# Roots of a norm moved to GpSimd, late additions behind a scaling, and weight splits held back, in a one-core trunk kernel

## The chip, the cores and the metric

The kernel runs on one core of a Trainium2 chip. Times are device microseconds; the metric is the median of several runs. The engines are TensorE (PE in the profile; PEld is its weight load), VectorE (DVE), ScalarE (ACT), GpSimd (POOL) and SyncE (SP), which issues the transfers.

## The reference, cut to what matters

One macaron layer over 1024 rows of 1024 columns, in float32: half a SwiGLU feed-forward, stick-breaking attention, half a SwiGLU feed-forward. Each has a root-mean-square norm in front.

```python
def rms_norm(x, gain):
    y = x * lax.rsqrt(jnp.mean(x * x, axis=-1, keepdims=True) + 1e-6)
    return y * gain

x = x + 0.5 * swiglu(rms_norm(x, l0_ff1_norm), l0_ff1_w_in, l0_ff1_w_out)   # w_in 1024x5632, w_out 2816x1024
x = x + stick_breaking_attention(rms_norm(x, l0_mix_norm), w_qkv, q_gain, k_gain, w_o)   # 16 heads of 64
x = x + 0.5 * swiglu(rms_norm(x, l0_ff2_norm), l0_ff2_w_in, l0_ff2_w_out)
```

The change concerns the second norm, `l0_mix_norm`, between the output product of the first feed-forward and the QKV product.

## The kernel before

Every float32 product is done as three fp32r products (`mm3`, lines 282 to 284): each operand is split into a high part, which ScalarE copies, and a low part, the difference, which VectorE or GpSimd takes (`split`, lines 185 and 186). Rows are handled in eight blocks of 128 ("row 0" to "row 7" below); the order is 4, 5, 6, 7, 0, 1, 2, 3, since the input comes reversed in time.

The output product of a feed-forward (`ffn_out`) is a Strassen-like scheme of seven half-size products, in the order 5, 1, 4, 3, 7, 2, 6 (`SEVEN`). A product has an inner length of 1408, in six chunks (`CHUNKS`): five of two 128-slices, one of one. For each chunk, transfers bring one or two parts of the weight into tiles `raw` and the stored gate product into `rh`; VectorE sums the weight parts where there are two (line 527); the splits write four tiles `rp`. Product 7 accumulates into four PSUM banks ma0 to ma3, product 2 into mb0 to mb3, product 6 again into ma. `result(t)` (line 573) adds a finished bank t, times 0.5 and a sign, into the residual `x_sb`, one addition for each half it goes to. Product 2 goes to two halves, so it has eight additions; they are the late ones: `finish_late` issues them behind a split of product 6's operands, by the table

```python
LATE = ((2, (0, 1)), (4, (2, 3)))
```

banks 0 and 1 behind chunk 2's last split, banks 2 and 3 behind chunk 4's. The last three chunks of product 6 are taken bank by bank (block 0 to block 3).

The hook `at` weaves the norm into these products. A norm of a row takes two squares with a sum on ScalarE (line 221), the sum of both halves `st` (line 230), the root `rsqrt` on VectorE (a scale-and-add, line 195; a first guess by integer arithmetic, line 198; three Newton steps of three instructions, lines 200 to 202), the scaling of the row by root and gain into `xs`, two instructions of 512 columns (line 245), and `turned`: eight transposes on TensorE into two banks (line 257) and the splits into `xh` and `xl`. Rows 4 and 5 are normed after product 7 and turned in product 2; rows 6 and 7 have their root taken in product 2, are scaled behind chunk 4's split of product 6, and are turned in banks mb0 to mb3 after block 0 of product 6. Rows 0 to 3 are normed one by one after blocks 0 to 3; row 0 is turned after block 3, row 1 after the first block of the QKV product, rows 2 and 3 after the fourth.

The QKV product of a head pair accumulates 128 rows by 384 columns in one of two banks `bq`, empties them (`sq`, `qk`, `vst`, lines 774 to 780) and goes on. `weights_of` loads its weights `raw_qkv` in four steps of two slices and splits them into `wqh` (ScalarE, line 742) and `wql` (GpSimd, line 745). The table `behind` names tiles that a step has to wait for: a GpSimd multiply of two columns (line 740) reads such a tile and writes where the split will write. For the first head pair, the first two steps (slices 4 to 7) wait for nothing, the other two for the last `xl` of row 7:

```python
for engine, to, f in behind[n]:
    there = f().to_broadcast([P, 2])
    engine.tensor_tensor((h_, l_)[to][:, ks, 0], there, there, op=ALU.mult)
```

The framework orders the instructions of each engine when the program is built, by the priorities of their place in the text and planned times; `issue_after` adds an edge of order to one engine's queue. At run time each engine goes through its queue in that order.

Of the kernel before, what the change touches and what calls it, by code (L numbers as in the profile page):

```python
# [9 lines left out]
F32 = mybir.dt.float32  # L10
# [3 lines left out]
ALU = mybir.AluOpType  # L14
# [3 lines left out]
P = 128  # L18
T = 1024
D = 1024  # L20
# [7 lines left out]
EPS = 1e-6  # L28
# [56 lines left out]

ON_POOL_H = {2: (1,), 6: (1, 3, 5)}

LATE = ((2, (0, 1)), (4, (2, 3)))

W_OF = {  # L90
    1: ((0, 0), (1, 1), "add"), 2: ((0, 0),), 3: ((0, 1), (1, 1), "subtract"), 4: ((1, 0), (0, 0), "subtract"),
# [17 lines left out]
def macaron_kernel(ctx, tc, x, g1, w1_in, w1_out, gm, w_qkv, gq, gk, w_o, g2, w2_in, w2_out, out):  # L109
    nc = tc.nc  # L110
    act, dve, pool_e, pe, sp = nc.scalar, nc.vector, nc.gpsimd, nc.tensor, nc.sync
# [62 lines left out]
    make_identity(nc, ident)  # L174
    xh = cpool.tile([P, KD, T], F32R, name="xh")
    xl = cpool.tile([P, KD, T], F32R, name="xl")
    above = cpool.tile([P, 104], F32, name="above")
    pool_e.memset(below, 0.0)
    pool_e.memset(above, 0.0)
    x_keep = [dram.tile([T, D], F32, name=f"x_keep{i}") for i in range(2)]  # L180
    o_keep = [dram.tile([NP * P, T], F32, name=f"o_keep{n}") for n in "hl"]

# [6 lines left out]
    def rsqrt(pool, ss, inv_n, y=None):  # L189
# [12 lines left out]
            dve.scalar_tensor_tensor(out=y, in0=u, scalar=1.5, in1=y, op0=ALU.subtract, op1=ALU.mult)  # L202
        return y

    def load_gain(pl, g):

        t = pl["xs"].tile([P, D], F32, name="gain", bufs=1)
        sp.dma_start(t, g.broadcast_to([P, D]))
        return t
# [10 lines left out]
                junk = pl["hs"].tile([P, NHALF], F32, name="hs", bufs=1)  # L220
                act.activation(junk, row(tb, h), AF.Square, accum_out=ss[:, i, h : h + 1])

    def rates(pl, row, tbs, ss=None):

        n = len(tbs)
        if ss is None:
            ss = pl["xs"].tile([P, n, 2], F32, name="ss")
            squares(pl, row, tbs, ss)
        st = pl["xs"].tile([P, n], F32, name="st")
        dve.tensor_tensor(st, ss[:, :, 0], ss[:, :, 1], op=ALU.add)  # L230
        return rsqrt(pl["xs"], st, 1.0 / D)

    def norm(pl, row, tbs, gain, ss=None, r=None, behind=None):

        if r is None:
            r = rates(pl, row, tbs, ss)
        turns = []  # L240
        for i, tb in enumerate(tbs):
            xs = pl["xs"].tile([P, D], F32, name="xs")
            with tc.issue_after(behind) if behind is not None else nullcontext():
                for h in range(2):
                    dve.scalar_tensor_tensor(
                        out=xs[:, HALVES[h]], in0=row(tb, h), scalar=r[:, i : i + 1], in1=gain[:, HALVES[h]],
                        op0=ALU.mult, op1=ALU.mult,
                    )
            turns.append(partial(turned, xs, tb))
        return turns  # L250
# [258 lines left out]
    def ffn_out(pl, w_out, keep, x_from, ahead, at):  # L509

        place["rp"] = 0
        x_sb = [pl[f"x{h}"].tile([P, NT, NHALF], F32, name=f"x{h}", bufs=1) for h in range(2)]

        def room(n):
            i = PLACES[place["rp"] % len(PLACES)]
            place["rp"] += 1  # L520
            return pl[f"rp{i}"].tile([P, 2, NHALF], F32R, name="rp", bufs=1)[:, :n]

        def operands(m, c):
            n = len(CHUNKS[c])
            *w, h = ahead.pop((m, c), None) or operand_raw(pl, w_out, keep, m, c)
            if len(w) == 2:
                dve.tensor_tensor(w[0], w[0], w[1], op=getattr(ALU, W_OF[m][2]))  # L527
            wh, wl, hh, hl = (room(n) for _ in range(4))
            marks = *split(w[0], wh, wl, pool_e), *split(h, hh, hl, pool_e if c in ON_POOL_H.get(m, ()) else dve)
            return (wh, wl), (hh, hl), marks  # L530

        def load(th, h):
            for tb in range(4 * (1 - th), 4 * (1 - th) + 4):
                sp.dma_start(x_sb[h][:, tb, :], x_from[rows(tb), HALVES[h]])

        def finish_late(m, result, ops, part):

            c, ts = LATE[part]
            for t in ts:
                with tc.issue_after(ops[c][2][3]):  # L540
                    result(t)
            with tc.issue_after(ops[-1][2][0]), tc.issue_after(ops[-1][2][2]):
                at(x_sb, m, f"end {part}", ops)

        open_banks = {}
        loaded = set()
        for m, tag, fresh, goes in SEVEN:
            last = m == SEVEN[-1][0]
            late = m == SEVEN[-2][0]
            if fresh:  # L550
                open_banks[tag] = [bank(tag) for _ in range(4)]
            bs = open_banks[tag]
            ops = [operands(m, c) for c in range(len(CHUNKS))]
            for (th, h), _ in goes:
                if (th, h) not in loaded:
                    load(th, h)
                    loaded.add((th, h))

            def add(ts, cs):
                for c in cs:  # L560
                    (wh, wl), (hh, hl), _ = ops[c]
                    for i, q in enumerate(CHUNKS[c]):
                        for t in ts:
                            s = slice(t * P, (t + 1) * P)
                            mm3(
                                bs[t], [((hh[:, i, s], hl[:, i, s]), (wh[:, i], wl[:, i]))],
                                fresh and q == 0, q == NQ - 1, not fresh,
                            )

            def result(t, bs=bs, goes=goes):  # L570
                for (th, h), sign in goes:
                    xc = x_sb[h][:, 4 * (1 - th) + t, :]
                    dve.scalar_tensor_tensor(out=xc, in0=bs[t], scalar=0.5 * sign, in1=xc, op0=ALU.mult, op1=ALU.add)

            if last:
                late_result(ops, 0)
            n = len(CHUNKS) - BY_BLOCK if last else len(CHUNKS)
            for c in range(n):
                add(range(4), [c])
                at(x_sb, m, c, ops)  # L580
                if last and c == 0:
                    late_result(ops, 1)
            for t in range(4):
                add([t], range(n, len(CHUNKS)))
                if not late:
                    result(t)
                if last:
                    at(x_sb, m, f"block {t}", ops)
            if late:
                late_result = partial(finish_late, m, result)  # L590
            else:
                at(x_sb, m, "end", ops)
# [25 lines left out]
    pending = []  # L618
    with pools(*RAWS) as pr:
        ops = {}  # L620
# [37 lines left out]
        late, stores = [], []  # L658
        norms = ExitStack()
        pn = norms.enter_context(pools("xs", "hs", side="right"))  # L660
        with banks("ps2"), pools(*SECOND) as pl:
            lay_banks()
            gain_m = load_gain(pn, gm)
            half = pn["xs"].tile([P, 4, 2], F32, name="half", bufs=1)

            def at(x_sb, m, where, ops):
                def row(tb, h):
                    return x_sb[h][:, tb, :]

                def store(tbs, hs):  # L670
                    for tb in tbs:
                        for h in hs:
                            sp.dma_start(x_keep[0][rows(tb), HALVES[h]], row(tb, h))

                def turn_rows(bk, n):
                    for _ in range(n):
                        pending.pop(0)(bk)

                if (m, where) == (7, "end"):
                    pending.extend(norm(pn, row, (4, 5), gain_m))  # L680
                    store((4, 5, 6, 7), (0, 1))
                elif (m, where) == (2, 2):
                    turn_rows("ma", 2)
                elif (m, where) == (2, 3):
                    late.append(rates(pn, row, (6, 7)))
                elif (m, where) == (6, 0):

                    pending.extend(norm(pn, row, (6, 7), gain_m, r=late.pop(), behind=ops[4][2][3]))
                elif m == 2 and str(where).startswith("end"):
                    ts = slice(*((0, 2), (2, 4))[int(where[-1])])  # L690
                    squares(pn, row, range(4)[ts], half[:, ts], (0,))
                elif m == 6 and str(where).startswith("block"):
                    t = int(where[-1])
                    turn_rows("mb", (2, 0, 0, 1)[t])
                    squares(pn, row, (t,), half[:, t : t + 1], (1,))
                    last_norm = lambda: pending.extend(norm(pn, row, (t,), gain_m, half[:, t : t + 1]))
                    if t < 3:
                        last_norm()
                    else:
                        late.append(last_norm)  # L700
                    stores.append(partial(store, (t,), (0, 1)))

            ffn_out(pl | pr, w1_out, keep, x, ops, at)

# [5 lines left out]
    with ExitStack() as stack:  # L710
# [228 lines left out]
        steps = qkv(0, states[0])  # L939

        last_x = ((pool_e, 0, lambda: xl[:, KD - 1, T - P : T - P + 1].bitcast(F32)),)
        for f in weights_of(0, states[0], ((), last_x)):
            f()
        with tc.issue_after(states[0]["loaded"]):
            for f in stores:
# [212 lines left out]
```

## Time and profile before

| | us |
|---|---|
| median of 3 runs | 1951.02 |
| lowest and highest | 1950.53, 1951.62 |
| profiled execution, its own time | 1951.8 |
| its span (first to last instruction) | 1950.0 |
| busy PE, PEld | 1910.0 (98%), 1639.0 (84%) |
| busy DVE, ACT, POOL | 1267.2 (65%), 986.9 (51%), 1092.4 (56%) |
| mean granted clock of TensorE | 0.999 |

A busy share is a mean over stages of different kinds. What the change touches lies between 603 us, where product 2 begins, and about 700 us, where the attention's scores are near; so the stretch and the single waits in it are to be read, and not the shares. In a timeline a line is one group of like instructions: start, duration of the group, engine, line, operation, tile written and tiles read, shape, count, and in brackets the idle time before it and what ended it.

### The profile page before, as it was taken

What the parts mean: (1) busy time and instruction counts of PE and PEld (TensorE: products, weight loads), DVE (VectorE), ACT (ScalarE), POOL (GpSimd) and SP (SyncE); (2) the same over time, 40 slices, a digit from 0 to 9 for tenths busy, and PEclk for the clock granted to TensorE, in tenths of its full rate; (3) what the DMA queues carried; (4) which work ended last, traced back from release to release, by engine and by line L of the source; (5) the groups of instructions that cost most, each with busy time, mean ns of one, the idle gap of its engine ahead of it and who ended that gap; (6) DMA issues with size and microseconds to landing.
All of it is one profiled execution on the core that took longest, in us unless ns stands there. A gap on an engine that the chain in (4) does not pass through costs nothing.

```text
span 1950.0 us, 27326 instructions
## 1 busy us (share of the span) xinstructions
PE 1910.0 (98%) x9656; PEld 1639.0 (84%) x9656; DVE 1267.2 (65%) x1834; ACT 986.9 (51%) x1802; POOL 1092.4 (56%) x963
## 2 busy tenths in 40 slices
PE   7999999999999999999999999999999999999998
PEld 7978888888888898888989897789888888888887
DVE  7855545635876867878787878475645545548644
ACT  6533443344334457777787877344433343343332
POOL 3667667655545636656655664113666666655554
PEclk9999999999999999999999999999999999999999
DMA  6223223338896411011011134521323232369973
GB/s 211 82 92 125 98 97 104 118 114 277 322 344 229 139 34 43 32 43 49 28 39 45 60 114 167 179 70 43 129 87 121 98 103 88 129 211 339 337 267 134
DMA packets 168505, 260.26 MB, mean 133 GB/s; under 512 B 11568, under 2 KB 81200, under 8 KB 168368
## 3 DMA queue, kind: packets, MB, share of 16 engines
q1 hardware_dynamic: 168368, 258.52, 38.8%
q8 instruction: 75, 1.23, 0.3%
q14 instruction: 62, 0.51, 0.1%
HBM read 198.18 MB, written 60.29 MB: 133 GB/s over the span
## 4 chain that ended last, share of the span: by engine, by line
PE 85%; DVE 8%; ACT 3%; issue 2%; POOL 2%; DMA 1%; DVEq 0%; POOLq 0%; ACTq 0%
PE ka L282 6%; PE ka L284 6%; PE ka L283 6%; PE kc L284 4%; PE kc L282 4%; PE kc L283 4%; PE kb L284 4%; PE kb L282 4%; PE kb L283 4%; PE ma L283 4%; PE ma L284 4%; PE ma L282 4%; PE bq L282 4%; PE bq L283 4%; PE bq L284 4%; PE bo L905 3%
## 5 line engine op out<-in xcount | busy, mean ns | idle before, releaser
L186 POOL TENSOR_TENSOR u<-sf,u 128x512 fp32r<-128x512 f32 x160 | 226.1, 1415 | 150.9 <-ACT u L185 147.0
L186 POOL TENSOR_TENSOR rp<-raw,rp 128x1024 fp32r<-128x1024 f32 x84 | 208.9, 2491 | 179.1 <-ACT rp L185 168.3
L186 POOL TENSOR_TENSOR u<-raw,u 128x512 fp32r<-128x512 f32 x136 | 196.2, 1448 | 164.2 <-ACT u L185 162.9
L185 ACT ACTIVATE u<-sf 128x512 fp32r<-128x512 f32 x160 | 100.7, 630 | 214.8 <-PE kb L283 86.8
L865 POOL TENSOR_TENSOR w<-w,om 128x512 f32<-128x512 f32 (+4 forms) x128 | 141.1, 1106 | 114.6 <-DVE om L858 88.3
L401 DVE TENSOR_TENSOR h<-h 128x512 f32<-128x512 f32 x110 | 135.4, 1234 | 85.9 <-POOL h L505 85.1
L282 PE MATMUL bq<-wqh,xh 128*128 128x384 f32 x512 | 174.8, 341 | 2.1 <-DVE vst L779 2.1
L284 PE MATMUL bq<-wqh,xl 128*128 128x384 f32 x512 | 172.2, 336 | 0.0
L283 PE MATMUL bq<-wql,xh 128*128 128x384 f32 x512 | 172.1, 336 | 0.0
L185 ACT ACTIVATE rp<-rh 128x1024 fp32r<-128x1024 f32 (+1 forms) x78 | 76.4, 984 | 188.0 <-issue 57.5
L282 PE MATMUL ka<-xh,u 128*128 128x512 f32 (+1 forms) x448 | 162.2, 362 | 1.5 <-ACT s L453 1.5
L283 PE MATMUL ka<-xl,u 128*128 128x512 f32 (+1 forms) x448 | 162.1, 362 | 0.0
L284 PE MATMUL ka<-xh,u 128*128 128x512 f32 (+1 forms) x448 | 161.9, 361 | 0.0
L527 DVE TENSOR_TENSOR raw<-raw 128x1024 f32<-128x1024 f32 (+1 forms) x60 | 97.6, 1629 | 99.0 <-DMA raw<-w_out 89.1
L185 ACT ACTIVATE u<-raw 128x512 fp32r<-128x512 f32 x136 | 84.9, 631 | 148.9 <-PE ka L283 101.2
L282 PE MATMUL ma<-rp 128*128 128x512 f32 x352 | 137.5, 390 | 0.0
L283 PE MATMUL ma<-rp 128*128 128x512 f32 x352 | 137.2, 390 | 0.0
L284 PE MATMUL ma<-rp 128*128 128x512 f32 x352 | 137.2, 390 | 0.0
L856 ACT ACTIVATE w<-bz,f 128x512 f32<-128x512 f32 (+2 forms) x192 | 112.5, 586 | 41.5 <-PE bz L852 38.9
L505 POOL TENSOR_TENSOR h<-h,g 128x512 f32<-128x512 f32 x80 | 113.0, 1412 | 35.1 <-DVE h L457 33.3
L430 DVE TENSOR_TENSOR sf<-raw 128x512 f32<-128x512 f32 x80 | 81.2, 1015 | 78.0 <-POOL u L186 77.9
L186 DVE TENSOR_TENSOR rp<-rh,rp 128x1024 fp32r<-128x1024 f32 (+1 forms) x70 | 106.2, 1535 | 22.6 <-ACT rp L185 19.7
(272 smaller groups left out, 5557.8 us busy)
## 6 DMA issues: line engine op xcount, KB each, us to landing
raw<-w_out SPq DMA_DIRECT2D x120, 512.0 KB, 5.4
raw<-w_in SPq DMA_DIRECT2D x88, 512.0 KB, 3.6
k<-h SPq DMA_DIRECT2D x154, 256.0 KB, 2.1
rh<-k SPq DMA_DIRECT2D x64, 512.0 KB, 5.8
raw_qkv<-w_qkv SPq DMA_DIRECT2D x64, 192.0 KB, 2.9
x_keep<-x SPq DMA_DIRECT2D x32, 256.0 KB, 3.7
x<-x_keep SPq DMA_DIRECT2D x32, 256.0 KB, 5.2
raw<-w_out SPq DMA_DIRECT2D x24, 256.0 KB, 4.7
```

What stands on the lines that cost most here:

```text
L185: act.activation(hi, raw, AF.Copy).ins,
L186: (engine or dve).tensor_tensor(lo, raw, hi.bitcast(F32), op=ALU.subtract).ins,
L282: pe.matmul(dst, ah, bh, start=start and i == 0, stop=False, skip_group_check=onto)
L283: pe.matmul(dst, ah, bl, start=False, stop=False, skip_group_check=onto)
L284: pe.matmul(dst, al, bh, start=False, stop=stop and i == n - 1, skip_group_check=onto)
L401: dve.tensor_tensor(src, hb[of[0]], hb[of[1]], op=getattr(ALU, of[2]))
L430: dve.tensor_tensor(f[n], x, y, op=op)
L505: pool_e.tensor_tensor(h, h, gs[k], op=ALU.mult)
L527: dve.tensor_tensor(w[0], w[0], w[1], op=getattr(ALU, W_OF[m][2]))
L856: act.activation(to, z, AF.Sigmoid, scale=state["f", half][:, sign, tb % 4, hd : hd + 1])
L865: pool_e.tensor_tensor(wt[:, c1 : c0 + n], wt[:, c1 : c0 + n], om[:, c1 - 1 : c0 + n - 1], op=ALU.mult)
L905: pe.matmul(ot[:, :n], vv, t[:, c : c + n], start=start, stop=stop)
```

## The change

All six roots of this norm (rows 4 and 5 together, 6 and 7 together, 0, 1, 2 and 3) go to GpSimd: the sum `st`, one scale-and-add, and one `tensor_tensor` with `pow` against a constant tile of -0.5 take the place of the twelve VectorE instructions. The other two norms keep `rsqrt`. The tile `above`, which only fills memory, shrinks by 8 columns as the tile `power` comes in. The late additions of banks 0 and 1 go from behind chunk 2's split to behind chunk 4's, and both parts are issued in the text after the scaling of rows 6 and 7. The first two weight steps of the first head pair get a wait on GpSimd for the first late addition of row 0 (`added`). `store` gets `row` as an argument, so that `added` can reach the tile.

```diff
-LATE = ((2, (0, 1)), (4, (2, 3)))
+LATE = ((4, (0, 1)), (4, (2, 3)))
...
-    above = cpool.tile([P, 104], F32, name="above")
+    above = cpool.tile([P, 96], F32, name="above")
+    power = cpool.tile([P, 1], F32, name="power")
...
+    pool_e.memset(power, -0.5)
...
+    def root(pool, ss, inv_n):
+        n = ss.shape[-1]
+        a, y = (pool.tile([P, n], F32, name=f"rs_{i}", bufs=b) for i, b in (("a", 4), ("y", 2)))
+        pool_e.tensor_scalar(a, ss, inv_n, EPS, op0=ALU.mult, op1=ALU.add)
+        pool_e.tensor_tensor(y, a, power.to_broadcast([P, n]), op=ALU.pow)
+        return y
...
-    def rates(pl, row, tbs, ss=None):
+    def rates(pl, row, tbs, ss=None, pooled=False):
...
-        dve.tensor_tensor(st, ss[:, :, 0], ss[:, :, 1], op=ALU.add)
-        return rsqrt(pl["xs"], st, 1.0 / D)
+        (pool_e if pooled else dve).tensor_tensor(st, ss[:, :, 0], ss[:, :, 1], op=ALU.add)
+        return root(pl["xs"], st, 1.0 / D) if pooled else rsqrt(pl["xs"], st, 1.0 / D)
...
-            if last:
-                late_result(ops, 0)
...
-                if last and c == 0:
-                    late_result(ops, 1)
+                if last and c < 2:
+                    late_result(ops, c)
...
-                    pending.extend(norm(pn, row, (4, 5), gain_m))
+                    pending.extend(norm(pn, row, (4, 5), gain_m, pooled=True))
...
-                    late.append(rates(pn, row, (6, 7)))
+                    late.append(rates(pn, row, (6, 7), pooled=True))
...
-                    last_norm = lambda: pending.extend(norm(pn, row, (t,), gain_m, half[:, t : t + 1]))
+                    last_norm = lambda: pending.extend(norm(pn, row, (t,), gain_m, half[:, t : t + 1], pooled=True))
...
-                    stores.append(partial(store, (t,), (0, 1)))
+                    stores.append(partial(store, row, (t,), (0, 1)))
...
-        for f in weights_of(0, states[0], ((), last_x)):
+        added = ((pool_e, 1, lambda: stores[0].args[0](0, 0)[:, 0:1]),)
+        for f in weights_of(0, states[0], (added, last_x)):
```

More of the change, by code (lines that the diff above doesn't have):

```diff
@@ L229, in rates, with norm @@
         st = pl["xs"].tile([P, n], F32, name="st")
-        dve.tensor_tensor(st, ss[:, :, 0], ss[:, :, 1], op=ALU.add)
-        return rsqrt(pl["xs"], st, 1.0 / D)
-    def norm(pl, row, tbs, gain, ss=None, r=None, behind=None):
+        (pool_e if pooled else dve).tensor_tensor(st, ss[:, :, 0], ss[:, :, 1], op=ALU.add)
+        return root(pl["xs"], st, 1.0 / D) if pooled else rsqrt(pl["xs"], st, 1.0 / D)
+    def norm(pl, row, tbs, gain, ss=None, r=None, behind=None, pooled=False):
         if r is None:
-            r = rates(pl, row, tbs, ss)
+            r = rates(pl, row, tbs, ss, pooled)
         turns = []
@@ L668, in row, with store @@
                     return x_sb[h][:, tb, :]
-                def store(tbs, hs):
+                def store(row, tbs, hs):
                     for tb in tbs:
@@ L679, in at @@
                 if (m, where) == (7, "end"):
-                    pending.extend(norm(pn, row, (4, 5), gain_m))
-                    store((4, 5, 6, 7), (0, 1))
+                    pending.extend(norm(pn, row, (4, 5), gain_m, pooled=True))
+                    store(row, (4, 5, 6, 7), (0, 1))
                 elif (m, where) == (2, 2):
```

## The prediction

> **What bounds the kernel now.** I read busy time by stretches first, to see where TensorE does not work; then its waits there; then the timelines of the four engines around each wait. A line of the first view: stretch, us, busy us and instructions of PE, PEld, DVE, ACT and POOL, granted clock, DMA share, GB/s.
>
> ```profile
> 600.00:640.00 40.00, 40.00 (x184) 33.01 (x184) 31.67 (x45) 22.42 (x36) 24.04 (x10) 1.00 0.66 223
> 640.00:700.00 60.00, 55.69 (x294) 49.56 (x293) 49.92 (x112) 26.02 (x58) 31.28 (x30) 0.97 0.35 110
> ...
> 800.00:900.00 100.00, 96.74 (x580) 88.88 (x579) 80.64 (x155) 77.75 (x168) 59.18 (x88) 1.00 0.13 40
> ```
>
> TensorE is the bound: from 600 to 640 us, where the first moved root lies, it never rests; from 640 to 700, where the other edits lie, it idles 60.00 - 55.69 = 4.3 us. Two waits, both for VectorE, make that up (waited for, total us, times, longest):
>
> ```profile
> PE mb L257 <- DVE x L573: 2.2, 2, 1.9
> PE bq L282 <- DVE vst L779: 2.1, 1, 2.1
> ```
>
> On TensorE's timeline (start, duration):
>
> ```profile
> 655.49 1.03 PE L257 MATMUL mb<-ident,xs 128*128 128x128 f32 x8
> 658.41 0.92 PE L257 MATMUL mb<-ident,xs 128*128 128x128 f32 x4 [1.90 <-DVE x L573]
> 659.61 1.11 PE L257 MATMUL mb<-ident,xs 128*128 128x128 f32 x4 [0.27 <-DVE x L573]
> 660.37 0.78 PE L282 MATMUL ma<-rp 128*128 128x512 f32 x1
> ...
> 662.16 0.40 PE L283 MATMUL ma<-rp 128*128 128x512 f32 x1
> 662.40 0.39 PE L284 MATMUL ma<-rp 128*128 128x512 f32 x1
> ...
> 671.48 1.03 PE L257 MATMUL mb<-ident,xs 128*128 128x128 f32 x8
> ...
> 681.22 0.33 PE L283 MATMUL bq<-wql,xh 128*128 128x384 f32 x1
> 681.39 0.34 PE L284 MATMUL bq<-wqh,xl 128*128 128x384 f32 x1
> 683.84 0.45 PE L282 MATMUL bq<-wqh,xh 128*128 128x384 f32 x1 [2.11 <-DVE vst L779]
> ```
>
> Stall 1: the 16 transposes of rows 6 and 7 take banks mb0 to mb3, four each. Eight go at once; mb2 and mb3 wait for the last late additions of product 2. No product runs from 655.49 to 660.37, 4.9 us. Stall 2: the third QKV block wants the bank of the first, which VectorE (vst) empties late; start to start that is 683.84 - 681.39 less the usual 0.17, 2.3 us.
>
> **Part 1, additions behind the scaling, weights' splits held.** VectorE, then GpSimd:
>
> ```profile
> 645.83 2.47 DVE L573 SCALAR_TENSOR_TENSOR x<-mb,x 128x512 f32<-128x512 f32 x4
> 648.23 0.75 DVE L527 TENSOR_TENSOR raw<-raw 128x512 f32<-128x512 f32 x1
> 648.90 2.31 DVE L186 TENSOR_TENSOR rp<-rh,rp 128x1024 fp32r<-128x1024 f32 x1
> 651.14 6.02 DVE L245 SCALAR_TENSOR_TENSOR xs<-x,rs_y,gain 128x512 f32<-128x512 f32 x4
> 657.08 2.47 DVE L573 SCALAR_TENSOR_TENSOR x<-mb,x 128x512 f32<-128x512 f32 x4
> ...
> 668.19 1.41 DVE L245 SCALAR_TENSOR_TENSOR xs<-x,rs_y,gain 128x512 f32<-128x512 f32 x2
> ```
>
> ```profile
> 646.01 2.43 POOL L186 TENSOR_TENSOR rp<-raw,rp 128x1024 fp32r<-128x1024 f32 x1 [2.31 <-ACT rp L185]
> 648.36 1.77 POOL L186 TENSOR_TENSOR rp<-rh,rp 128x512 fp32r<-128x512 f32 x1
> 650.09 2.28 POOL L186 TENSOR_TENSOR rp<-raw,rp 128x512 fp32r<-128x512 f32 x1
> 652.45 5.57 POOL L745 TENSOR_TENSOR wql<-raw_qkv,wqh 128x384 fp32r<-128x384 f32 x4
> 662.85 0.34 POOL L740 TENSOR_TENSOR wqh<-xl 128x2 fp32r<-128x2 f32 x2 [4.84 <-DVE st L230]
> 664.01 3.94 POOL L745 TENSOR_TENSOR wql<-raw_qkv,wqh 128x384 fp32r<-128x384 f32 x4 [0.81 <-ACT wqh L742]
> 677.46 1.69 POOL L740 TENSOR_TENSOR wqh<-qk 128x2 fp32r<-128x2 f32 x4 [9.51 <-ACT qk L775]
> 679.34 3.91 POOL L745 TENSOR_TENSOR wql<-raw_qkv,wqh 128x384 fp32r<-128x384 f32 x4 [0.19 <-ACT wqh L742]
> ```
>
> A scaling (two SBUF tiles in) costs 6.02 / 4 = 1.5 us while GpSimd splits, and 1.41 / 2 = 0.7 at 668.19 while it rests. An addition (one bank, one SBUF tile) costs 2.47 / 4 = 0.62 with GpSimd busy or not. The change puts the additions, not the scaling, beside the first weights' splits.
>
> New order from 645.8: L527 0.75, chunk 4's split 2.31, to 648.9; scaling; eight additions, 8 x 0.62 = 4.9. With scaling at 4 x 0.7 the additions end at 656.6, with 4 x 1.5 at 659.8, against 659.55 now. GpSimd still has chunk 5's two splits, by its rows to 652.4, and after them only the held weights. I take contention till then: 3.5 / 1.5 = 2.35 pieces, 1.65 more at 0.7, so 653.6, and the additions end at 658.5. Four transposes follow, about 0.5 (half of the eight's 1.03) instead of 0.76: products resume at 659.05, **1.3 us earlier**. Between the ends that is 3.2 us and nothing.
>
> Behind the new wait on GpSimd (two multiplies of two columns, 0.34 / 2 = 0.17 each at 662.85) are the four first splits: released at about 654 and uncontended (3.94 for four), they end at 658, as now, so their second loads come no later. The next four wait for xl of row 7, as now, and come with it.
>
> A second gain is the clock:
>
> ```profile
> 659.00:660.00 1.00, 0.73 (x4) 0.39 (x3) 1.00 (x2) 0.95 (x3) 0.00 (x0) 0.50 0.47 129
> ...
> 681.70:683.90 2.20, 0.09 (x2) 0.06 (x1) 2.17 (x5) 0.83 (x3) 1.54 (x2) 1.00 0.44 122
> ```
>
> The 4.9 us without a product ended at half the granted clock; four products from 660.37 took 1.79 in place of 4 x 0.24, **0.8 lost**. The 2.3 us of stall 2 cost no clock. 659.05 - 655.49 = 3.6 lies between the two; I count half, 0.4 (ends 0 and 0.8). The Trainium skill, "TensorE: Matmul & The Clock Gate", section What's actually happening, has the clock halved after an idle window of about 3.4 us that runs free of the program. By that rule a gap of 4.9 would catch a whole window in 1.5 / 3.4 = 0.44 of executions and one of 3.6 in 0.06, an estimate of 0.38 x 0.8 = 0.3 saved on the median, and the sum would be 0.1 longer. The trace agrees as far as it goes: 0.50 after 4.9 us, 1.00 after 2.3.
>
> **Part 2, six roots to GpSimd.** Each takes twelve small instructions from VectorE and puts three on GpSimd. Around stall 2 and the first root:
>
> ```profile
> 613.36 0.15 DVE L230 TENSOR_TENSOR st<-ss 128x2 f32<-128x2 f32 x1
> ...
> 618.83 2.74 DVE L245 SCALAR_TENSOR_TENSOR xs<-x,rs_y,gain 128x512 f32<-128x512 f32 x4
> ...
> 676.66 0.15 DVE L230 TENSOR_TENSOR st<-half 128x1 f32<-128x1 f32 x1
> ...
> 679.47 0.90 DVE L202 SCALAR_TENSOR_TENSOR rs_y<-rs_u,rs_y 128x1 f32<-128x1 f32 x1
> ...
> 683.51 0.28 DVE L779 TENSOR_TENSOR vst<-bq,vst 128x128 fp32r<-128x128 f32 x1
> ```
>
> ```profile
> 677.26 0.28 ACT L778 ACTIVATE vst<-bq 128x128 fp32r<-128x128 f32 x1
> ```
>
> vst's input is there at 677.5; it starts at 683.51 because row 3's root stands before it, its last steps 0.9 us each beside the splits at 679.34. Without the chain vst can run by 679 with row 2's scaling ahead of it, and TensorE asks at 681.6: **2.3 us saved**. Next late would be the second block's vst, asked for one block (4 us) later.
>
> Price on GpSimd: sum and scale-and-add at 0.17 to 0.2; the power is in no row. I take 0.2, the row of the same shape; the upper end is 2.4, its longest operand split here of 1024 columns. A root is then X = 0.6 to 2.8 us. The first root:
>
> ```profile
> 608.95 3.40 POOL L186 TENSOR_TENSOR rp<-raw,rp 128x1024 fp32r<-128x1024 f32 x1 [3.47 <-ACT rp L185]
> 613.53 2.44 POOL L186 TENSOR_TENSOR rp<-raw,rp 128x1024 fp32r<-128x1024 f32 x1 [1.18 <-ACT rp L185]
> ...
> 624.02 2.40 POOL L186 TENSOR_TENSOR rp<-raw,rp 128x1024 fp32r<-128x1024 f32 x1 [5.83 <-ACT rp L185]
> ```
>
> It runs from 612.35, and the four scalings end at 613 + 2.8 = 616 instead of 621.6. Splits behind it shift by X into the 5.8 us idle before 624.02; so does the second root. At 2.8 both still fit. TensorE turns these rows at 620.0, so nothing is gained there either. For rows 0 to 3, blocks end at 662.4, 665.9 and 669.3 (three in 671.48 - 660.37 - 0.8 = 10.3 us): result 0.7, squares 0.8, root 0.6 and scaling 1.4 need 3.5, and TensorE turns row 0 at 669.3, row 1 a QKV block later. The weights' splits at 664.01 may stand behind two of these roots: they end at 667.95 - 1.3 + 2X, and QKV starts at 670.1, so 2X up to 3.4 is free, and 2.2 would be lost at X = 2.8. The memset of one column at the start (no input) and the shorter pad cost nothing; no DMA is added, and the stores keep their places in SP's queue.
>
> The Trainium skill, "GPSIMD Engine Reference", section Instruction dispatch, speaks against this part: the first call of freshly loaded code waits about 6 us. No run here shows it. By that the first root would end at about 619 and the scaling at 620.4 for row 4, an estimate of 0.7 us of TensorE's time lost; the forecast would be 1947.7.
>
> **Sum.** The profiled execution took 1951.8 (span 1950.0), 0.8 above the median 1951.02, and had the clock loss whole: 1951.8 - 1.3 - 0.8 - 2.3 = 1947.4. On the median: 1951.0 - 1.3 - 0.4 - 2.3 = **1947.0**. Everything later hangs on TensorE and shifts with it.
>
> **Rivals.**
> - One stall stays (0.20). VectorE's order is fixed when the program is built; if row 3's scaling comes ahead of vst and its root sits on GpSimd behind the splits of 679.34 to 683.25, stall 2 stays: 1951.0 - 1.7 = 1949.3. For: vst was put last now too. Against: these splits are traced later than the root. If scaling stays contended throughout, stall 1 stays: 1948.7.
> - Nothing comes out (0.10): the attention gives it back, 1951.0. For: TensorE idles 3.3 of 100 us there (800 to 900), in an order that may be planned anew. Against: those waits follow its own products.
> - Slower (0.12): the power is a long program. Past X = 1.7 each us costs 2 before QKV; at X = 3.7 the gain is gone, at 5.7 the time is 1955. Against: the short GpSimd rows of 0.17.
>
> **How the numbers follow.** The forecast has 0.58, its own range 1944.7 (3.2 + 0.8 + 2.3 saved) to 1948.8. About 0.2%, 3.9 us, is what a measurement can tell, so 1947.1 parts faster from same: some six tenths of the forecast's share, 0.37, is faster; its rest, one stall, and nothing make 0.49 same; the long power and a bad new order 0.14. The range 1944.6 to 1952.0 leaves out little below and the long power above.
>
> **What would show it.** Scaling of rows 6 and 7 at 0.7 to 1.1 us a piece, then eight additions in a row; TensorE's wait before the mb transposes under 1 us each, granted clock 1.00 there; no wait of bq for vst at 680; three GpSimd instructions per root at 0.2 each. Wrong if the power shows above 1.7 us, or bq waits for wql or xl.

## The result, and the profile after

The changed kernel takes 1945.95 us (median of 9 runs, 1945.13 to 1947.17), the kernel before 1951.02 on the same chip (9 runs, 1948.92 to 1953.22): a ratio of 0.9974 with an interval of 0.9964 to 0.9984. It takes 5.1 us less, a quarter of a percent, and the interval leaves out no change; the forecast of 1947.0 is 1.1 us above it. The profiled execution took 1945.95 (span 1944.2), against 1951.8 (span 1950.0).

Line numbers have moved: the split is now L188, the scaling L255, the transposes L267, the products L292 to L294, the additions L583, vst L787, the wait and the split of the weights L748 and L753; a root on GpSimd is L240, L211 and L212 (in the runs with more powers most of these are one further). The stretches that bound the kernel, in the columns of the prediction's first view:

```profile
600.00:640.00 40.00, 40.00 (x186) 33.37 (x185) 25.95 (x21) 22.63 (x36) 28.60 (x16) 1.00 0.68 233
640.00:700.00 60.00, 57.70 (x311) 51.41 (x310) 39.80 (x67) 27.18 (x61) 34.35 (x45) 1.00 0.33 103
```

TensorE idles 2.3 us from 640 to 700 where it idled 4.3, at the full granted clock. Its waits there (waited for, total us, times, longest):

```profile
PE mb L267 <- DVE x L583: 1.8, 4, 0.5
PE bt L267 <- DVE xl L188: 0.5, 1, 0.5
```

The wait of bq for vst is gone, the wait of the mb transposes is 1.8 in four pieces instead of 2.2 in two, and one wait is new: the transposes of row 1 (bt) for the splits of row 0. TensorE's timeline, of after and then, at the same places, of before:

```profile
620.88 0.48 PE L292 MATMUL mb<-rp 128*128 128x512 f32 x1
...
654.08 0.39 PE L294 MATMUL ma<-rp 128*128 128x512 f32 x1
654.65 0.66 PE L267 MATMUL mb<-ident,xs 128*128 128x128 f32 x4 [0.18 <-DVE x L583]
...
658.24 0.66 PE L267 MATMUL mb<-ident,xs 128*128 128x128 f32 x4 [0.54 <-DVE x L583]
658.65 0.47 PE L292 MATMUL ma<-rp 128*128 128x512 f32 x1
...
669.77 0.42 PE L292 MATMUL bq<-wqh,xh 128*128 128x384 f32 x1
...
674.68 1.23 PE L267 MATMUL bt<-ident,xs 128*128 128x128 f32 x8 [0.47 <-DVE xl L188]
675.66 0.42 PE L292 MATMUL bq<-wqh,xh 128*128 128x384 f32 x1
...
679.91 0.33 PE L292 MATMUL bq<-wqh,xh 128*128 128x384 f32 x1
```

```profile
622.03 0.47 PE L282 MATMUL mb<-rp 128*128 128x512 f32 x1
...
672.27 0.42 PE L282 MATMUL bq<-wqh,xh 128*128 128x384 f32 x1
...
677.31 0.42 PE L282 MATMUL bq<-wqh,xh 128*128 128x384 f32 x1
```

Subtracting pair by pair gives where the time came from. The turn of rows 4 and 5 begins 0.79 us earlier than before, a lead from ahead of the first moved root; after it (620.88 against 622.03) the lead is 1.15: 0.36 gained in the turn, where the kernel before has 0.4 us of waiting for the scaling and this one none. The products resume 1.72 earlier (658.65 against 660.37), so the gap around the mb transposes gave 0.54 to 0.57. Some 0.35 of that is the clock too: the last four transposes and the step to the first product took 660.37 - 659.61 = 0.76 at half clock before, and 658.65 - 658.24 = 0.41 now. QKV starts 2.50 earlier (669.77 against 672.27): 0.78, the half clock that did not come behind the gap. The second block starts only 1.65 earlier (675.66 against 677.31): 0.85 given back at the turn of row 1. The third block starts 3.93 earlier (679.91 against 683.84): 2.28, stall 2. By the last product the lead is 4.7, by the end of the span 5.8; the last 1.1 lies behind the last product, among the stores. From the start of the last product to the end it is 5.3 us in both profiles of the kernel before and with order and hold alone, and 4.1 to 4.2 in all ten others, one with its roots on VectorE among them; what sets it stays open.

VectorE and GpSimd of after:

```profile
645.26 3.41 DVE L188 TENSOR_TENSOR rp<-rh,rp 128x1024 fp32r<-128x1024 f32 x1
648.60 4.80 DVE L255 SCALAR_TENSOR_TENSOR xs<-x,rs_y,gain 128x512 f32<-128x512 f32 x4
653.32 4.86 DVE L583 SCALAR_TENSOR_TENSOR x<-mb,x 128x512 f32<-128x512 f32 x8
...
668.48 1.41 DVE L255 SCALAR_TENSOR_TENSOR xs<-x,rs_y,gain 128x512 f32<-128x512 f32 x2 [4.30 <-POOL rs_y L212]
669.82 1.28 DVE L583 SCALAR_TENSOR_TENSOR x<-ma,x 128x512 f32<-128x512 f32 x2
672.52 1.42 DVE L255 SCALAR_TENSOR_TENSOR xs<-x,rs_y,gain 128x512 f32<-128x512 f32 x2 [1.42 <-POOL rs_y L212]
673.85 1.28 DVE L188 TENSOR_TENSOR xl<-mb,xh 128x512 fp32r<-128x512 f32 x2
...
675.38 0.28 DVE L787 TENSOR_TENSOR vst<-bq,vst 128x128 fp32r<-128x128 f32 x1
```

```profile
612.77 0.20 POOL L211 TENSOR_SCALAR rs_a<-st 128x2 f32<-128x2 f32 x1
613.05 0.71 POOL L212 TENSOR_TENSOR rs_y<-rs_a,power 128x2 f32<-128x2 f32 x1
...
661.03 0.19 POOL L240 TENSOR_TENSOR st<-half 128x1 f32<-128x1 f32 x1 [1.51 <-ACT hs L231]
661.31 0.19 POOL L211 TENSOR_SCALAR rs_a<-st 128x1 f32<-128x1 f32 x1
661.59 0.55 POOL L212 TENSOR_TENSOR rs_y<-rs_a,power 128x1 f32<-128x1 f32 x1
...
663.25 4.13 POOL L753 TENSOR_TENSOR wql<-raw_qkv,wqh 128x384 fp32r<-128x384 f32 x4 [0.28 <-ACT wqh L750]
667.34 0.19 POOL L240 TENSOR_TENSOR st<-half 128x1 f32<-128x1 f32 x1
...
671.39 0.19 POOL L240 TENSOR_TENSOR st<-half 128x1 f32<-128x1 f32 x1 [2.94 <-ACT hs L231]
```

vst of the first block is at 675.38 where it was at 683.51. Read the rest as one chain, since each engine goes through its queue in order: row 1's root stands behind the four weights' splits of 663.25; VectorE waits 4.30 us for it and has row 2's addition (669.82) queued behind row 1's scaling; row 2's root needs that addition's squares; VectorE waits 1.42 us for that root, and row 0's splits (673.85) are queued behind row 2's scaling; for these splits the transposes of row 1 wait. That is the new wait. It is no price of GpSimd's alone: with order and hold but all roots on VectorE (second experiment) the same turn waits 0.51 us.

### The profile page after: what moved, and what is told of

Same layout as the page of the kernel before. It is cut to its first block, busy times and chain, and to the rows that moved or that the text cites. A ratio compares the mean times of both kernels' runs of the same rounds, so it can differ in the third digit from the quotient of the medians.

```text
span 1944.2 us, 27283 instructions
## 1 busy us (share of the span) xinstructions
PE 1906.9 (98%) x9656; PEld 1636.9 (84%) x9656; DVE 1253.4 (64%) x1762; ACT 985.7 (51%) x1802; POOL 1099.6 (57%) x984
## 4 chain that ended last, share of the span: by engine, by line
PE 85%; DVE 7%; ACT 3%; POOL 2%; issue 2%; DMA 1%; SPq 0%; DVEq 0%; POOLq 0%; ACTq 0%
PE ka L292 6%; PE ka L293 6%; PE ka L294 6%; PE kc L293 4%; PE kc L292 4%; PE kc L294 4%; PE kb L293 4%; PE kb L292 4%; PE kb L294 4%; PE ma L294 4%; PE ma L292 4%; PE ma L293 4%; PE bq L292 4%; PE bq L293 4%; PE bq L294 3%; PE mb L294 3%
## 5 line engine op out<-in xcount | busy, mean ns | idle before, releaser
L188 POOL TENSOR_TENSOR u<-sf,u 128x512 fp32r<-128x512 f32 x160 | 225.8, 1413 | 151.2 <-ACT u L187 147.3
L188 POOL TENSOR_TENSOR rp<-raw,rp 128x1024 fp32r<-128x1024 f32 x84 | 208.6, 2488 | 175.8 <-ACT rp L187 162.8
L188 POOL TENSOR_TENSOR u<-raw,u 128x512 fp32r<-128x512 f32 x136 | 195.9, 1446 | 164.0 <-ACT u L187 162.8
L292 PE MATMUL bq<-wqh,xh 128*128 128x384 f32 x512 | 174.6, 341 | 0.0
L294 PE MATMUL bq<-wqh,xl 128*128 128x384 f32 x512 | 172.1, 336 | 0.0
L292 PE MATMUL ka<-xh,u 128*128 128x512 f32 (+1 forms) x448 | 161.8, 362 | 2.0 <-ACT s L463 1.5
L294 PE MATMUL ka<-xh,u 128*128 128x512 f32 (+1 forms) x448 | 161.3, 360 | 0.0
L292 PE MATMUL ma<-rp 128*128 128x512 f32 x352 | 137.1, 389 | 0.0
L294 PE MATMUL ma<-rp 128*128 128x512 f32 x352 | 137.0, 389 | 0.0
L188 DVE TENSOR_TENSOR rp<-rh,rp 128x1024 fp32r<-128x1024 f32 (+1 forms) x70 | 111.5, 1610 | 22.1 <-ACT rp L187 19.4
```

The lines of the kernel that those rows point to most:

```text
L188: (engine or dve).tensor_tensor(lo, raw, hi.bitcast(F32), op=ALU.subtract).ins,
L292: pe.matmul(dst, ah, bh, start=start and i == 0, stop=False, skip_group_check=onto)
L294: pe.matmul(dst, al, bh, start=False, stop=stop and i == n - 1, skip_group_check=onto)
```

## The experiments

Two theories stood at the start. One: the roots carry the gain, and order and hold only move contention (theory B of the first recorded texts). The other: each part carries about the share that the prediction gave it, some 1.7 us for the order with its clock and 2.3 for the roots (their theory A). The letters in the later recorded texts are each text's own. Unless said otherwise an edit starts from the changed kernel.

**Roots alone.** The table of late additions, their place and the weights' waits are put back as before.

```diff
-LATE = ((4, (0, 1)), (4, (2, 3)))
+LATE = ((2, (0, 1)), (4, (2, 3)))
...
-        for f in weights_of(0, states[0], (added, last_x)):
+        for f in weights_of(0, states[0], ((), last_x)):
```

> The changed kernel with the additions and the first weights' splits where they were before: only the roots are on GpSimd. Theory A (two separate stalls, each cured by its own part): TensorE still waits 1.9 us and more before the transposes of rows 6 and 7 with 4.9 us between products, scaling at 1.5 us a piece; the wait of bq for vst at 681 is gone; 2.3 us saved, 1948.7 us. Theory B (the roots carry all, since VectorE has less to do everywhere): as the changed kernel, 1946 us, and the wait before these transposes is short too. Theory C (order and hold carry it): as before, 1951 us.

Measured: 1946.47 us, ratio 0.9979 (0.997 to 0.9988), all of the gain within the interval. VectorE's timeline, then TensorE's:

```profile
644.62 2.47 DVE L583 SCALAR_TENSOR_TENSOR x<-mb,x 128x512 f32<-128x512 f32 x4
...
647.68 2.32 DVE L188 TENSOR_TENSOR rp<-rh,rp 128x1024 fp32r<-128x1024 f32 x1
649.92 6.04 DVE L255 SCALAR_TENSOR_TENSOR xs<-x,rs_y,gain 128x512 f32<-128x512 f32 x4
655.88 2.47 DVE L583 SCALAR_TENSOR_TENSOR x<-mb,x 128x512 f32<-128x512 f32 x4
```

```profile
654.42 0.39 PE L294 MATMUL ma<-rp 128*128 128x512 f32 x1
...
658.82 0.48 PE L292 MATMUL ma<-rp 128*128 128x512 f32 x1
```

The scaling is as slow as before (6.04) and chunk 4's split as fast (2.32); the additions end at 658.35 against 658.18 with the new order. From block 0's last product (0.23 after the start of its row) the gap is 658.82 - 654.65 = 4.2 us, with the new order 658.65 - 654.31 = 4.3. The order shifts 1.1 us of contention from the scaling to the split and gains nothing here. The time is that of theory B, but not its short wait: TensorE still waits 2.1 us before the mb transposes, in pieces of 1.5 and 0.5. What is gone is the wait for vst, and the half clock.

**Order and hold alone.** `pooled=True` is taken out of the three calls, so all roots are on VectorE.

> The changed kernel with all roots back on VectorE: only the late additions' place and the held splits differ from before. Theory A: the gap between products at rows 6 and 7 is 4.3 us as in the changed kernel, TensorE waits under 1 us at a time there, no half clock; the wait of bq for vst stays at 2 us or more: 1.3 to 1.7 us saved, 1949.5 us. Theory B: 1951 us. Theory C: 1946 us.

Measured: 1951.47 us, ratio 1.0001 (0.9992 to 1.001). A wait of TensorE and VectorE's rows before it:

```profile
PE bq L292 <- DVE vst L787: 2.4, 1, 2.4
```

```profile
681.12 0.91 DVE L204 SCALAR_TENSOR_TENSOR rs_y<-rs_u,rs_y 128x1 f32<-128x1 f32 x1
...
682.87 0.28 DVE L787 TENSOR_TENSOR vst<-bq,vst 128x128 fp32r<-128x128 f32 x1
```

Stall 2 stays whole, with vst behind the Newton steps. TensorE reached QKV 1.88 us sooner than in the kernel before (670.39 against 672.27, with no half clock in the gap), but vst came only 0.64 sooner, so the stall, and a half clock behind it that the kernel before did not have there, took the lead back. With the roots on VectorE, then, nothing of the order's part is left at the end, and with the roots on GpSimd the order adds nothing that can be measured: for the time, the roots carry the gain.

**No hold.** Only the first weights' wait for `added` is taken out.

> The changed kernel without the wait of the first two weight steps for the first late addition. Theory A (GpSimd's splits double the scaling): GpSimd goes on splitting from 651.5, the scaling ends 1 us later (5.9 us for four instead of 4.8), all four banks come free 1 us later: 1 us over the changed kernel, 1947 us. Rival (order alone matters, the hold is idle): 1946.0 us and the gap between products at 4.3 us.

Measured: 1946.43 us, ratio 0.9979 (0.997 to 0.9988); the scaling took 4.80 us, as with the hold. The hold does nothing that these runs can tell.

**The turns of rows 6 and 7 later**, after blocks 1 and 2 of product 6 instead of both after block 0. They no longer ask for banks that are not emptied yet; the second weight steps' wait goes from row 7 to row 6.

```diff
-                    turn_rows("mb", (2, 0, 0, 1)[t])
+                    turn_rows("mb", (0, 1, 1, 1)[t])
...
-        last_x = ((pool_e, 0, lambda: xl[:, KD - 1, T - P : T - P + 1].bitcast(F32)),)
+        last_x = ((pool_e, 0, lambda: xl[:, KD - 1, T - 2 * P : T - 2 * P + 1].bitcast(F32)),)
```

> The changed kernel with rows 6 and 7 turned one at a time, after block 1 and block 2 of product 6 instead of both after block 0, and the wait of the last two weight steps put on row 6. Theory A: the additions have 3.4 us more to free the banks, TensorE does not wait at all there; of the 4.3 us without a product the 1.6 us of transposes remain, so 2.7 us less than the changed kernel, 1943.3 us. Rival (the wait goes to the next place): row 6's xl comes later, so the last weight splits and with them the first QKV block come later, TensorE waits there for wql, and the time is 1945 to 1946.5.

**And row 1's turn later too**, three steps on in the QKV product; by the trace that is one block on, 8.4 us after QKV's start instead of 4.9.

```diff
-            if i == 2:
+            if i == 5:
                 pending.pop(0)("bt")
                 late.pop()()
-            elif i in (5, 7, 9, 11):
+            if i in (5, 7, 9, 11):
```

> The kernel with the spread turns (rows 6 and 7 after blocks 1 and 2), and row 1 turned after the second QKV block instead of the first, row 3's norm behind it. Theory D (the wait of bt for xl that came with the roots on GpSimd is a debt of their queue: row 2's root stands behind four weight splits, VectorE waits for it with row 0's xl behind): TensorE has no wait left from 610 to 690, 0.6 us less than with the spread turns alone, 1944.1 us. Rival (row 3's scaling now waits for row 1's tile and holds vst up): a wait of bq for vst of 1 us or more, 1945 to 1946 us.

Measured: 1944.72 us with the first edit (ratio 0.9968, 0.9957 to 0.998) and 1942.89 with both (0.9954, 0.994 to 0.9968). The stretch from 640 to 700, of the first and of both:

```profile
640.00:700.00 60.00, 59.50 (x325) 53.90 (x324) 40.12 (x68) 27.32 (x61) 35.47 (x45) 1.00 0.34 107
```

```profile
640.00:700.00 60.00, 59.97 (x332) 54.95 (x331) 41.83 (x68) 27.39 (x62) 35.93 (x44) 1.00 0.32 99
```

Each edit takes away the wait it aims at: first the 1.8 us before the mb transposes, then the 0.5 before bt. With both TensorE does not wait from 600 to 700, and the runs lie within 1942.85 to 1943.74. The second is below every run of both kernels. With the first edit 2.7 us less than the changed kernel was expected and 1.2 came. In its profile, of an execution 2.3 us above its median, the stretch from the turn of rows 4 and 5 to QKV's start is 2.6 shorter, but half clocks from 20 to 40 and from 1188 to 1192 us, far from the edit, took most of it back.

**Both later turns, roots back on VectorE** (`pooled=True` out of the three calls). Are the roots on GpSimd still needed then?

> The later turns (rows 6 and 7 one block later, row 1 three QKV blocks later) with the changed order and the hold, but all six roots back on VectorE as in the kernel before. Theory: the moved turns remove the transposes' wait (1.5 to 2.1 us) whoever takes the roots, but the stall of the third QKV block for vst (2.35 us) comes from the Newton chain on VectorE and stays, so about 1951.0 - 2 - 0.5 = 1948.5 us, some 5.5 us above the same kernel with the roots on GpSimd (1942.9). Rival: the turns were all that was needed and the roots are hidden once the turns are later: within 1.5 us of 1942.9, and no wait of bq for vst.

Measured: 1952.99 us, ratio 1.0006 (0.9997 to 1.0015): 10.1 us above the same kernel with its roots on GpSimd (1942.89), where 5.5 was expected. (Row 1's turn is three steps later here too, which is one QKV block and not three.) TensorE's wait, and VectorE ahead of it:

```profile
PE bq L292 <- DVE vst L787: 4.8, 1, 4.8
```

```profile
679.77 2.85 DVE L255 SCALAR_TENSOR_TENSOR xs<-x,rs_y,gain 128x512 f32<-128x512 f32 x2
...
683.72 0.28 DVE L787 TENSOR_TENSOR vst<-bq,vst 128x128 fp32r<-128x128 f32 x1
```

With the turns late the chains of rows 2 and 3 and a scaling that GpSimd's splits slow to 2.85 all stand ahead of vst; the stall doubles, and the mean granted clock from 680 to 700 is 0.83. The later turns pay only with the roots on GpSimd.

**Both later turns, roots on GpSimd, order as before and no hold** (the first experiment's edit on top of the two turns).

> The later turns and the roots on GpSimd, with the late additions' places and the first weights' splits as in the kernel before (no hold). Theory (order and hold only shift contention between scaling and split): same time as with them, 1942.9 within 1.5 us, and no wait of the mb transposes. Rival: with the turns later, the additions of all eight being late matters: the time differs by 2 us or more one way or the other.

Measured: 1943.21 us, ratio 0.9954 (0.9942 to 0.9967), the same as with order and hold, and no wait before the mb transposes either. Order and hold can be left out.

**Five powers in each root, two powers in each root, and powers of four sizes.**

```diff
-        pool_e.tensor_tensor(y, a, power.to_broadcast([P, n]), op=ALU.pow)
+        for _ in range(5):
+            pool_e.tensor_tensor(y, a, power.to_broadcast([P, n]), op=ALU.pow)
```

With `range(2)` in place of `range(5)` it is done twice. The repeats write the same values again.

> The changed kernel with the power of each root done five times (the same result), about 0.55 us each by the changed kernel's trace, so a root of 3.2 to 4 us instead of 1. Theory by the prediction: free up to 1.7 us a root, then 2 us per us, since two roots stand before the splits that the first QKV block needs: 3 us or more lost, 1949 us or more. Theory D: rows 1 and 2 hang on each other through VectorE's queue (row 1's scaling, row 2's addition and squares, row 2's root, row 0's xl, row 1's turn), so the 2.2 us more count twice at the turn in bt, from the start: 4.4 us, 1950.4 us, and the wait is seen on bt, not on bq. Rival (hidden): 1946 us.

> The changed kernel with the power done twice in each root (the second writes the same values again). One root grows by 0.55 us for one row and 0.7 to 1.1 us for two rows. The prediction's price (free up to a root of 1.7 us): roots of one row go from 0.95-1.65 to 1.5-2.2 us, so next to nothing, 1946 to 1947. Rival, a chain in which row 1's root stands behind four weight splits and row 0's root: the wait of the bt transposes grows from 0.5 by about 2 x 0.55 to 1.6 us, and the time to about 1947.5; with five powers it was 15 us, that is 3.7 us for each added power, so 1949.7 if the price is proportional.

Measured: 1960.82 us with five (ratio 1.0044, 1.003 to 1.0059) and 1949.36 with two (0.9992, 0.9983 to 1.0001). A wait of TensorE with five, its turn of row 1 and the start of row 0's root; then the same two places with two:

```profile
PE ma L295 <- DVE rp L188: 3.7, 1, 3.7
```

```profile
687.73 1.94 PE L268 MATMUL bt<-ident,xs 128*128 128x128 f32 x8 [7.92 <-DVE xl L188]
```

```profile
666.65 0.19 POOL L241 TENSOR_TENSOR st<-half 128x1 f32<-128x1 f32 x1 [1.49 <-ACT hs L232]
```

```profile
677.57 1.23 PE L268 MATMUL bt<-ident,xs 128*128 128x128 f32 x8 [0.79 <-DVE xl L188]
```

```profile
662.02 0.19 POOL L241 TENSOR_TENSOR st<-half 128x1 f32<-128x1 f32 x1 [1.52 <-ACT hs L232]
...
662.58 1.19 POOL L213 TENSOR_TENSOR rs_y<-rs_a,power 128x1 f32<-128x1 f32 x2
```

The chain read above holds three roots in a row: row 0's, ahead of the splits; row 1's, behind them; row 2's, behind row 1's scaling. So a longer power counts three times at the bt transposes. With two powers, from row 0's root to those transposes it is 677.57 - 662.02 = 15.55 against 674.68 - 661.03 = 13.65: 1.9 us more, and three times the added 0.6 is 1.8. With five it is 687.73 - 666.65 = 21.08, 7.4 more; three times four added powers of 0.61 is 7.3. That settles the count of three, where the expectation had two.

The times hold more than the chain. With five powers 15 us are lost, where 3 or more, or 4.4, were expected. In the profiles QKV starts 5.6 later, the first block with the turn of row 1 takes 8.1 more, and a half clock behind that wait costs 1.7. The 3.7 us wait is a second place: an operand of product 6, which VectorE splits beside GpSimd's splits, and these stand 4.5 later (634.41 against 629.89) behind the second root of two rows. With two powers the median is 3.4 above the changed kernel, nearest to the 1949.7 scaled from five, but the profile does not put that down to the chain: of the 2.9 us by which its span is longer, 1.0 is there already at the turn of rows 4 and 5, 1.6 is the half clock in and behind the mb gap, and the wait for bt grows by 0.3 only, since TensorE itself comes later. Whether the 1.0 and the half clock are the program's or chance stays open.

The sizes are run in place before the first product, on a tile of twos that nothing reads, each k columns wide, with one multiply of the whole tile behind them:

```diff
+        for k in (1, 8, 32, 96):
+            pool_e.tensor_tensor(above[:, :k], above[:, :k], power.to_broadcast([P, k]), op=ALU.pow)
+        pool_e.tensor_tensor(above, above, power.to_broadcast([P, 96]), op=ALU.mult)
```

> The changed kernel with five more instructions on GpSimd where it idles before the attention: the power on 1, 8, 32 and 96 columns of a tile and a product on 96. It tells what the power costs by itself. If the power is a program per element: 0.55 us at 1 column rising steeply, 3 us or more at 96. If it is a fixed cost: under 1 us at all sizes. The product on 96 columns: 0.35 us by the row of 127 columns in the attention. Time as the changed kernel, 1946 us.

The program put them at the very start, not late in the norm, so the 1956.69 us of its one run is no price of the change (TensorE waits 12.5 us for GpSimd there); the durations are what it gives. Groups of the tile: count, shortest, median and longest ns, first and last start; the first two powers, the third, all four, the multiply:

```profile
L973 POOL TENSOR_TENSOR above<-above,power x2: 560/1106/1652, 1.4 to 2.1; 128x1 f32<-128x1 f32 x1, 128x8 f32<-128x8 f32 x1
```

```profile
L973 POOL TENSOR_TENSOR above<-above,power x1: 5424/5424/5424, 3.8 to 3.8; 128x32 f32<-128x32 f32 x1
```

```profile
L973 POOL TENSOR_TENSOR above<-above,power x4: 560/3538/15711, 1.4 to 9.3; 128x1 f32<-128x1 f32 x1, 128x8 f32<-128x8 f32 x1, 128x32 f32<-128x32 f32 x1, 128x96 f32<-128x96 f32 x1
L974 POOL TENSOR_TENSOR above<-above,power x1: 345/345/345, 25.1 to 25.1; 128x96 f32<-128x96 f32 x1
```

0.56, 1.65, 5.42 and 15.71 us for 1, 8, 32 and 96 columns: about 0.4 and 0.16 a column, while a multiply of 96 columns takes 0.345.

**The kernel before, profiled once more.**

> The kernel before, once more, for a second profile. Its times lie in two groups, near 1949.6 and near 1953. Theory E (chance halvings of the clock behind its two stalls): the wait times are the same as in the first profile, and the halved stretch is elsewhere or missing; without it 1951 us. Rival: one of the waits, or a transfer, differs by 2 us or more.

Measured: 1951.02 us in one run. TensorE's row of stall 2, and the granted clock (third figure from the end) behind the mb gap here and with two powers:

```profile
683.23 0.44 PE L282 MATMUL bq<-wqh,xh 128*128 128x384 f32 x1 [1.15 <-DVE vst L779]
```

```profile
660.00:661.00 1.00, 1.00 (x5) 0.93 (x4) 0.86 (x3) 1.00 (x3) 0.00 (x0) 0.50 0.95 282
```

```profile
660.00:661.00 1.00, 1.00 (x5) 0.81 (x4) 1.00 (x2) 1.00 (x3) 0.50 (x1) 0.50 0.94 262
```

The gap ended at half clock again, and the wait of bq for vst was 1.15 us instead of 2.11: the size of stall 2 differs from run to run, its place does not. This execution took the median time, as the changed kernel's profiled one did, so the two are the fairer pair. The same subtraction there gives 0.9 us ahead of the change, 0.36 at the turn of rows 4 and 5, 0.55 in the gap, 1.04 of clock behind it, 0.85 given back at row 1's turn, 1.33 for stall 2, and some 1.7 behind the third block, 1.1 of it behind the last product.

## Why the prediction was right, and where its steps were not

The direction and the mechanism of the larger part were right, and the total came within 1.1 us. Step by step:

- **Stall 2, 2.3 us.** The mechanism was right: the wait comes and goes with the roots alone (0.9979 with them, 1.0001 without). The size is 2.28 against the profile that the forecast was read from, and 1.33 against the second one, so that 2.3 on the median was not shown. The next late thing, though, was named wrongly. Not the second block's vst: the turn of row 1 came first, 0.85 us given back ahead of the gain.
- **Scaling 4.7, additions 4.9, gap 1.3 shorter.** The two durations came out (4.80 and 4.86; a scaling of 1.2 a piece, just above the 0.7 to 1.1 named as a sign), the gain did not: 0.54 to 0.57 in the profile. The step that failed is chunk 4's split, kept at its traced 2.31. Moved ahead of the additions it ran beside GpSimd's split of 1024 columns (2.76 us) and took 3.41, and the 1.1 us so lost is nearly what the scaling won. Of the half microsecond 0.35 is clock, and the run with the roots alone has as short a gap (4.2 us, 4.3 with order alone, 4.9 before), so none of it was shown to be the order's.
- **Clock, 0.4 on the median, 0.8 in the profile.** The profile shows the 0.78 behind the gap, and 0.35 more within it, which the prediction counted as part of the 1.3. That it belongs to the order was not shown: the run with two powers has the new order and a half clock in the same gap. The halving is a matter of the run, as the prediction's half count supposed, but nothing shows its odds changed.
- **Power at 0.2 by the row of the same shape.** Mis-sized: 0.55 for one column and 0.71 to 1.09 for two. The root was 1.1 us for rows 0 and 1 and 2.2 to 2.5 for the pairs, inside the range of 0.6 to 2.8.
- **Free up to a root of 1.7, then 2 per us, in front of QKV.** Wrong. QKV's start did not wait for wql; the chain of three roots ended at the turn of row 1, which waited 0.5 us already, so there was no slack left and the chain's price there is 3 per us. The long power's own run shows it: five powers, a root of 3.6 us in row 0 (0.19, 0.19, 3.04 and the steps between), lengthen the chain by 7.4 us and cost 15 in all, where the prediction had no gain lost until 1.7 and the 4.0 of it gone at 3.7. The place was missed because each root was weighed by what stands ahead of it on GpSimd, and not by what VectorE has queued behind the instruction that waits for it.
- **Nothing gained at 620.** 0.36 was: before, the transposes of rows 4 and 5 waited 0.4 for their scaling.
- **First call.** The first power took 0.71 us and started 0.08 after the instruction before it. The Trainium skill, "GPSIMD Engine Reference", section Instruction dispatch, has about 6 us for the first call of freshly loaded code; neither this trace nor the sizes' run, where the first power started at 1.44, shows any such wait.

So the total holds partly by compensation, which is luck. The profiled executions differ by 5.85 us where the sum had 4.4: 2.28 for stall 2 as forecast, 0.78 of clock, 0.54 for the gap (0.35 of it clock) instead of 1.3, 0.85 lost at row 1's turn, and four gains that were in no term: 0.79 ahead of the first moved root and 1.1 behind the last product, both away from the change, 0.36 at 620, and 0.75 between the third block and the last product. By the medians the roots alone make 1951.1 into 1946.5; how that gain divides between stall 2 (1.3 to 2.3), fewer half clocks and the rest stays open within the intervals, some 2 us to either side. Of the rivals, the one with a stall left was half right: the first stall stayed (1.8 us of waits), and the time was made up elsewhere.

## What to carry to other kernels

When a step moves to another engine, follow the instruction that waits for it on the old engine and list what is queued behind that one: that chain, not the moved step's own queue, sets what the step may cost, and steps that depend on each other through it count several times. When contention makes one instruction slow, moving it away hands the contention to whatever stands there next, so add up the whole group. Where a transpose waits for a bank or an operand, asking for it a block or two later can be worth as much as making the operand earlier, provided nothing else is then pushed into a later stall.

## What the runs showed of the hardware

- A power on GpSimd costs by the element: 0.16 us a column of 128 rows, against at most 0.0036 for a multiply (0.345 / 96). For a root of one or two columns that is small; for a tile of 96 it is 15.7 us.
- Small VectorE instructions, 0.16 us by themselves, take 0.90 to 1.02 beside GpSimd's splits, and a scaling of two pieces 2.85 instead of 1.41; additions with one input in a bank are not slowed (4.86 / 8 = 0.61).
- The half clock. In the gap around the mb transposes it came in three profiles (both of the kernel before, gaps of 4.9 us, and two powers, 4.7) and not in four (the changed kernel, roots alone, order alone, no hold, 3.8 to 4.3). With two powers the transposes waited 0.54 each as in the changed kernel, and the last four of them ran at half clock already, which is the difference of 0.4: the same gap was halved in one run and not in another. With order and hold alone the clock fell to 0.50 after stall 2, a wait of 2.35 us, as it did not in the kernel before after 2.11 and 1.15. Halvings also fall far from the change: over 20 to 40 us the mean granted clock is 0.91 in two profiles (the kernel before profiled once more, and the later turns of rows 6 and 7), over 1180 to 1200 us in two (these turns, and no hold), and 1.00 in the others. The Trainium skill, "TensorE: Matmul & The Clock Gate", section What's actually happening, has the halving follow a whole idle window of about 3.4 us that runs free of the program. That gaps of one length differ from run to run agrees; a halving after 2.35 us does not.
- Over all its runs the kernel before scatters over 6.5 us (1948.8 to 1955.3), the two versions with later turns and roots on GpSimd, ten runs in all, over 1.0. They have no wait from 600 to 700 where a halving could start; that this is the reason was not shown.
